# Low weight parts kept in DRAM for the second token half, and weight pieces subtracted in two halves of 256 columns

## The chip, the cores and the metric

The kernel runs on one core of a Trainium2 chip. The metric is the device time of one execution in microseconds (us); three executions of the kernel before took 2840.0, 2847.2 and 2849.79 us, median 2847.2. A core has five engines that run side by side, each through its own instructions in program order: TensorE (PE; its weight loads are shown apart as PEld), VectorE (DVE), ScalarE (ACT), GpSimd (POOL) and SyncE (SP), which here issues every DMA.

## What is computed

One layer of a hybrid encoder trunk over 1024 tokens of width 2048. A combined projection of the normalized input feeds two branches: a recurrent mixer with 16 heads (RWKV-7) and a sparse attention that lets each query see its 256 best-scored keys. Their gated outputs go through an output projection, then a gated update with a side input `p` and a final norm.

```python
def reference(x, p, w_in, norm_g, ...):
    h = x
    xn = rms_norm(h, norm_g[i])
    z = xn @ w_in[i]
    z_rw, g_rw, q_lat, kv_lat, k_idx, w_idx, g_ds = jnp.split(z, splits, axis=-1)
    o_rw = rwkv7_mixer(z_rw, ...)          # state S updated token by token
    o_ds = dsa_mixer(q_lat, kv_lat, k_idx, w_idx, ...)   # top_k(score, 256), softmax over those
    mixed = jnp.concatenate([o_rw * jax.nn.silu(g_rw), o_ds * jax.nn.silu(g_ds)], axis=-1)
    h = h + mixed @ w_out[i]
    h = h + (p[i] @ ple_w[i]) * jax.nn.sigmoid(h @ ple_gate_w[i])
    return rms_norm(h, final_g)
```

## The kernel before

**Split products.** Every large matrix product is taken in three matmuls, so that the fast number format of TensorE (`F32R`) loses nothing: a float32 operand is split into a high part (its rounded copy) and a low part (the difference), and the product is `wh*xh + wh*xl + wl*xh`. `w_piece` (line 507) does this for a weight piece of 128 x 512 values (four blocks of 128 x 128): a DMA loads it into `wr`, ACT makes `wh` by a copy, POOL makes `wl` by a subtraction of 512 columns, and `gemm_part` (line 517) runs twelve matmuls of 128 x 512 on it. `wr` has four buffers and `wh` and `wl` five each (`NWR, NWH`). The weight of the combined projection, `w_z` (46 column tiles of four pieces) with `w_z80` (one narrow tile of four pieces), makes 188 pieces. It goes through `w_piece` twice, once for each half of the tokens (`hf` 0 and 1, 512 tokens each): PE holds the split `x` of one half at a time (`xh`, `xl`).

**Phase 1, to about 1.6 ms.** For each token half, eight units of two heads: `zunit` projects their four tiles (r, k, v, gate), and two steps of 256 tokens each (`sub`, line 960) run the recurrence: `chunk_setup` builds and inverts small triangular matrices on PE, DVE, ACT and POOL, `chunk_serial` walks four chunks of 64 tokens. The steps are a chain, each waiting for the state of the one before. Between them stands work that nobody waits for soon, at the lowest priority (`LF`): in the second half these are `dsa_lat(1)`, the eight gate tiles `gds(j, 1)`, and behind the units the first thirteen tiles of the output projection of the recurrent branch for the first token half, `wout_rw(0)` (`MW`, matmuls on `mh`, `ml`).

**Phase 2, to about 2.27 ms.** It can begin when the last step has left its buffers. `pix` matmuls score all keys for 16 index heads; DVE adds them up in `MK`. Then a search on DVE and ACT halves an interval 31 times for each group of query tiles (`count`, `jk` on DVE and `js` on ACT, line 1146), and `pick_keys` marks the keys. The rest of `wout_rw` (three tiles of the first token half, sixteen of the second) is the work that PE has beside scoring and search. Then come the attention heads in eight pairs `u`, whose logits are the `plg` matmuls; those of query tiles 2 to 7 need the search.

**Phase 3.** The other half of the output projection, the gated update and the norm, again with `w_piece` (`w_o`, `w_pg`, `w_pl`).

**What sets the order.** Nothing is issued as it is written. `Sched` records all operations, and `plan` (line 267) lays them out engine by engine with costs and latencies of its own: the engine that is free first takes the ready operation of the lowest level number (chain of the recurrence 0, weight splits and evacuations 1, scoring 2, projections 3, `LF` 4). A POOL operation with operands in SBUF is planned as one that excludes DVE operations with two such operands, and the other way round (`lock`). Line 382 issues the result, so nearly every instruction of the profile carries that line and is known by its tiles. An engine runs its instructions in that fixed order, whatever the true times are.

Of the kernel before, what the change touches and what calls it, by code (L numbers as in the profile page):

```python
# [10 lines left out]
F32 = mybir.dt.float32  # L11
# [4 lines left out]
OP = mybir.AluOpType  # L16
# [12 lines left out]
LB, LA, LC, LEVAC, LSPLIT, LX, LG, LF, LSQ = 0, 0, 1, 1, 1, 2, 3, 4, 4  # L29
# [356 lines left out]
def hybrid_kernel(ctx, tc, cst, msk, bkt, prm, xt, pt_, w_z, w_z80, w_lora, w_uq, w_iq, w_uk, w_uv, w_o, w_pg,  # L386
                  w_pl, rel_bias, out):
    ctx.enter_context(tc.manual_schedule())
    nc = Sched(tc.nc)
    dram = ctx.enter_context(tc.tile_pool(name="dram", bufs=1, space=DRAM))  # L390
    dt = lambda n, shape: dram.tile(shape, F32, name=n)
# [2 lines left out]
    kid = [dt(f"ki{h}", [64, TH]) for h in range(2)]  # L394
    gdd, h1d = ([[dt(f"{n}{j}_{h}", [128, TH]) for h in range(2)] for j in range(m)] for n, m in (("gd", 8), ("h1", 16)))
    bsk, vbd = dt("bsk", [16, 128, 384]), dt("vb", [16, 384])
    parts = {}

    def pool(stack, keep=None, **kw):
        p_ = Pool(nc, stack.enter_context(tc.tile_pool(**kw)), kw["bufs"])  # L400
# [106 lines left out]
    def w_piece(src, kn, n):  # L507
        wr = wp.tile([128, 4, 128], F32, name="wr", tag="wr", bufs=W_[0])
        nc.sync.dma_start(wr[:, :kn, :n], src.rearrange("p (k n) -> p k n", k=kn))
        with nc.level(LSPLIT):  # L510
            wh = wp.tile([128, 4, 128], F32R, name="wh", tag="wh", bufs=W_[1])
            nc.scalar.activation(wh[:, :kn, :n], wr[:, :kn, :n], AF.Copy)
            wl = wp.tile([128, 4, 128], F32R, name="wl", tag="wl", bufs=W_[1])
            nc.gpsimd.tensor_tensor(wl[:, :kn, :n], wr[:, :kn, :n], wh[:, :kn, :n], op=OP.subtract)
        return wh, wl

    def gemm_part(pz, src, n, k0, kn, nk, xh, xl, w=None):
        wh, wl = w or w_piece(src, kn, n)
        for k in range(kn):
            kk = k0 + k  # L520
            for j, (a, b) in enumerate(((wh, xh), (wh, xl), (wl, xh))):
                nc.tensor.matmul(pz[:n], a[:, k, :n], b(kk), start=(kk == 0 and j == 0),
                                 stop=(kk == nk - 1 and j == 2), skip_group_check=True)
# [16 lines left out]
    def zgroup(tiles, before=lambda g, piece: None):  # L540
        pzs = [pz_tile() for _ in tiles]
        for g in range(4):
            early = []
            before(g, lambda: early.append(w_piece(w_z[tiles[len(early)], g], 4, 128)))
            for j, (pz, i) in enumerate(zip(pzs, tiles)):
                gemm_part(pz, w_z[i, g], 128, g * 4, 4, 16, xh_, xl_, early[j] if early else None)
        return pzs
# [363 lines left out]
    def kept(n, g):  # L911

        if (n, g) in parts:
            pair = []
            for d, nm in zip(parts[n, g], ("wh", "wl")):
                t = wp.tile([128, 4, 128], F32R, name=nm, tag=nm, bufs=W_[1])
                nc.sync.dma_start(t.bitcast(F32), d)
                pair.append(t)
            return pair
        pair = w_piece(w_o[n, g], 4, 128)  # L920
        parts[n, g] = [dt(f"wo{n}_{g}{a}", [128, 4, 128]) for a in "hl"]
        for d, t in zip(parts[n, g], pair):
            nc.sync.dma_start(d, t.bitcast(F32))
        return pair
# [605 lines left out]
```

## Time and profile before

| | us |
|---|---|
| executions timed | 2840.0, 2847.2, 2849.79 |
| median | 2847.2 |
| the profiled execution | 2844.57 |
| its span in the profile | 2842.8 |
| PE busy | 2701.8 (95%) |
| DVE busy | 1644.8 (58%) |
| ACT busy | 1482.0 (52%) |
| POOL busy | 1336.5 (47%) |

The profile is of one execution. Busy time of PE is a union of matmul spans that overlap each other: a stretch that is 100% busy is read for its number of matmuls. The 1.8 us between the profiled execution and its span lie outside the first and last instruction.

### The profile page before, as it was taken

To read this page: it belongs to the slowest core of one execution; us is meant where nothing else is said; L and a number is where in the kernel's file an instruction comes from. 1 tells how busy PE (TensorE), PEld (TensorE's weight loads), DVE (VectorE), ACT (ScalarE), POOL (GpSimd) and SP (SyncE) were. 2 spreads that over 40 slices of the span, in tenths; PEclk is the share of its full clock that TensorE was granted. 3 is DMA by queue.
4 is the path that set the end of the run, shared out by engine and by line. 5 is a ranking of instruction groups with operands and counts; after the bars stand their busy time and mean duration, and the time that the engine had idled before them with its cause. 6 is when DMAs were issued, how large, how long until landed. Compare 5 with 4: busy or idle time off the path is not lost. (4 is left out here: it accounts for less than half of the span.)

```text
span 2842.8 us, 46633 instructions
## 1 busy us (share of the span) xinstructions
PE 2701.8 (95%) x16482; PEld 2157.9 (76%) x16482; DVE 1644.8 (58%) x3709; ACT 1482.0 (52%) x3265; POOL 1336.5 (47%) x1371
## 2 busy tenths in 40 slices
PE   7999999999999999999999999948999999999996
PEld 5777778778778778777877788826776788878885
DVE  6457667546764566667665478987666641135312
ACT  5445555535654355555555466895767533343332
POOL 5545445555455545545555421023334455656654
PEclk9999999999999999999999999968999999999998
DMA  4232222232332222222227844511223343355332
GB/s 159 82 116 70 68 71 75 75 89 71 99 100 84 89 68 68 71 69 70 79 82 240 310 146 137 175 36 39 73 65 90 102 138 97 97 157 174 103 99 92
DMA packets 172586, 293.36 MB, mean 103 GB/s; under 512 B 23440, under 2 KB 44992, under 8 KB 172352
## 3 DMA queue, kind: packets, MB, share of 16 engines
q1 hardware_dynamic: 172352, 290.38, 32.9%
q8 instruction: 130, 2.13, 0.3%
q14 instruction: 104, 0.85, 0.1%
HBM read 232.87 MB, written 52.19 MB: 100 GB/s over the span
## 5 line engine op out<-in xcount | busy, mean ns | idle before, releaser
L382 POOL TENSOR_TENSOR wl<-wr,wh 128x512 fp32r<-128x512 f32 (+1 forms) x624 | 812.8, 1306 | 773.5 <-ACT wh L382 720.4
L382 ACT ACTIVATE wh<-wr 128x512 fp32r<-128x512 f32 (+1 forms) x624 | 384.1, 617 | 731.7 <-PE pz L382 536.1
L382 PE MATMUL pz<-xh,wh 128*128 128x512 f32 (+1 forms) x1504 | 609.5, 407 | 11.5 <-ACT wh L382 7.6
L382 PE MATMUL pz<-xh,wl 128*128 128x512 f32 (+1 forms) x1504 | 610.2, 408 | 2.3 <-POOL wl L382 2.1
L382 PE MATMUL pz<-xl,wh 128*128 128x512 f32 (+1 forms) x1504 | 611.1, 408 | 0.0
L382 PEld LDWEIGHTS pz<-xh,wh 128*128 128x128 f32 (+1 forms) x1504 | 285.6, 190 | 62.5 <-ACT wh L382 9.4
L382 PEld LDWEIGHTS pz<-xh,wl 128*128 128x128 f32 (+1 forms) x1504 | 285.1, 190 | 51.4 <-POOL wl L382 5.5
L382 PEld LDWEIGHTS pz<-xl,wh 128*128 128x128 f32 (+1 forms) x1504 | 285.8, 190 | 45.9 <-DVE xl L382 0.3
L382 DVE SCALAR_TENSOR_TENSOR tg<-tg,pg 128x512 f32<-128x512 f32 x32 | 22.0, 687 | 314.3 <-ACT tg L382 303.1
L382 DVE CAST_PREDICATED QX<-MS,pq 128x512 f16<-128x512 uint8 x160 | 110.3, 689 | 158.7 <-PE pq L382 157.6
L382 PE MATMUL pz<-hh,wh 128*128 128x512 f32 x512 | 199.3, 389 | 0.0
L382 PE MATMUL pz<-hh,wl 128*128 128x512 f32 x512 | 199.3, 389 | 0.0
L382 PE MATMUL pz<-hl,wh 128*128 128x512 f32 x512 | 199.2, 389 | 0.0
L382 POOL TENSOR_TENSOR mb<-mk,bt 128x256 f32<-128x256 f32 (+1 forms) x128 | 89.2, 702 | 153.6 <-DVE mx L382 126.3
L382 ACT ACTIVATE Ztb<-pzt 64x256 f16<-64x256 f32 x320 | 120.6, 377 | 61.3 <-PE pzt L382 55.9
L382 ACT ACTIVATE lgt<-lgt,nm 128x128 f32<-128x128 f32 (+7 forms) x128 | 98.8, 772 | 55.0 <-DVE nm L382 54.2
L382 PE MATMUL ptt<-C,lgt 128*128 128x128 f32 x576 | 99.7, 289 | 23.8 <-ACT lgt L382 22.4
L382 ACT ACTIVATE Sw<-UV,Wx 64x64 f32<-64x64 f32 x240 | 82.2, 342 | 58.9 <-DVE UV L382 55.5
L382 PEld LDWEIGHTS pz<-hh,wh 128*128 128x128 f32 x512 | 96.1, 188 | 20.0
L382 PEld LDWEIGHTS pz<-hl,wh 128*128 128x128 f32 x512 | 96.1, 188 | 20.0
L382 PEld LDWEIGHTS pz<-hh,wl 128*128 128x128 f32 x512 | 96.1, 188 | 19.7
L382 PE MATMUL po<-PT,V 128*64 128x128 f32 x1152 | 87.6, 287 | 18.7 <-ACT PT L382 18.2
(331 smaller groups left out, 6008.3 us busy)
## 6 DMA issues: line engine op xcount, KB each, us to landing
wr<-in_w_z_dram SPq DMA_DIRECT2D x368, 256.0 KB, 2.6
wr<-in_w_pg_dram SPq DMA_DIRECT2D x128, 256.0 KB, 2.6
wr<-in_w_o_dram SPq DMA_DIRECT2D x88, 256.0 KB, 2.9
h<-h SPq DMA_DIRECT2D x60, 256.0 KB, 3.2
h<-in_xt_dram SPq DMA_DIRECT2D x32, 256.0 KB, 3.7
out_dram<-h SPq DMA_DIRECT2D x32, 256.0 KB, 2.3
gd<-gd SPq DMA_DIRECT2D x16, 256.0 KB, 2.3
mix<-m SPq DMA_DIRECT2D x32, 128.0 KB, 1.7
```

Of the source, the lines that this page charges most:

```text
L382: getattr(self.real[o.eng], o.name)(*o.args, **o.kw)
```

## The change

Two edits, both in `w_piece`.

```diff
-    parts = {}
+    parts, lows, KEEP = {}, {}, (w_z.tensor.name, w_z80.tensor.name)
...
             wl = wp.tile([128, 4, 128], F32R, name="wl", tag="wl", bufs=W_[1])
-            nc.gpsimd.tensor_tensor(wl[:, :kn, :n], wr[:, :kn, :n], wh[:, :kn, :n], op=OP.subtract)
+            key = src.tensor.name, src.offset
+            if key in lows:
+                nc.sync.dma_start(wl[:, :kn, :n].bitcast(F32), lows[key])
+                return wh, wl
+            for k in range(0, kn, 2):
+                k_ = slice(k, min(k + 2, kn))
+                nc.gpsimd.tensor_tensor(wl[:, k_, :n], wr[:, k_, :n], wh[:, k_, :n], op=OP.subtract)
+        if src.tensor.name in KEEP:
+            lows[key] = dt(f"low{len(lows)}", [128, kn, n])
+            with nc.level(LF):
+                nc.sync.dma_start(lows[key], wl[:, :kn, :n].bitcast(F32))
         return wh, wl
```

The first time a piece of `w_z` or `w_z80` comes by (first token half), its `wl` is also stored to a DRAM tile of 256 KB, at the lowest level. The second time, `wl` is loaded from there and POOL does nothing for it; `wr` is still loaded and `wh` still made by ACT. All pieces that POOL still subtracts, of every weight with `kn` above 2, are subtracted in two operations of 256 columns each. The matmuls are the same in number and shape.

The planner lays all of this out anew. On POOL, in the second token half, the weight pieces stood between the operations of the recurrence (`IX`, `rsd`, `hr`, `QX`, `BRb`, `rk`, `ALb`, `Wx`). One step before:

```order
L382 TENSOR_TENSOR wl<-wr,wh 128x512 x3
L382 TENSOR_TENSOR IX<-C,QX 128x256
L382 COPY zt<-carry 128x1
L382 TENSOR_TENSOR rsd<-vr,nh 128x4
L382 TENSOR_TENSOR wl<-wr,wh 128x512
L382 TENSOR_TENSOR hr<-hs,nh 128x4
L382 COPY QX<-eye_178 128x512
L382 TENSOR_TENSOR wl<-wr,wh 128x512
L382 TENSOR_TENSOR BRb_218<-r,Wx 64x4x64 x2
L382 TENSOR_TENSOR wl<-wr,wh 128x512 x3
L382 TENSOR_TENSOR rk<-r,kp 128x256
L382 TENSOR_TENSOR wl<-wr,wh 128x512
```

and after:

```order
L382 TENSOR_TENSOR IX<-C,QX 128x256
L382 TENSOR_TENSOR rsd<-vr,nh 128x4
L382 COPY zt<-carry 128x1
L382 TENSOR_TENSOR hr<-hs,nh 128x4
L382 COPY QX<-eye_178 128x512
L382 TENSOR_TENSOR BRb_218<-r,Wx 64x4x64 x2
L382 TENSOR_TENSOR rk<-r,kp 128x256
L382 TENSOR_TENSOR ALb_211<-AB,A16b_217 64x4x64 x2
```

The operations of the recurrence now follow each other with no weight piece between them. On SP, at the same place, each load of a raw piece had no partner before:

```order
L382 DMA wr<-in_w_z_dram 128x512 x7
L382 DMA upr<-in_w_lora_dram 128x256
L382 DMA wr<-in_w_z_dram 128x512 x3
L382 DMA mix_2_69<-m 128x256
L382 DMA wr<-in_w_z_dram 128x512 x15
```

and after:

```order
L382 DMA wl<-low_964 128x512
L382 DMA wr<-in_w_z_dram 128x512
L382 DMA wl<-low_968 128x512
L382 DMA wr<-in_w_z_dram 128x512
L382 DMA upr<-in_w_lora_dram 128x256
L382 DMA wl<-low_1125 128x512
L382 DMA wr<-in_w_z_dram 128x512
```

Loads of `wl` and `wr` alternate; the `wr` behind a `wl` is that of a piece three further on. On PE the change shows at the end of the scoring. Before, the last `pix` matmuls are followed by the output projection of the second token half (`mh_19066`, `mh_19072`), 186 matmuls, up to the first `pg<-CH,hk` of the attention:

```order
L382 MATMUL pz<-mh_19072,wl 128x512
L382 MATMUL pix<-KIH,qs_19036 128x512
L382 MATMUL pix<-KIL,qs_19036 128x512
L382 MATMUL pix<-KIH,qs_19036 128x512
L382 MATMUL pix<-KIL,qs_19036 128x512
L382 MATMUL pz<-mh_19066,wh 128x512
L382 MATMUL pz<-ml_19067,wh 128x512
```

After, the output projection of the first token half (`mh_4064`, `mh_4070`) is not done yet when the scoring ends, and all of the second half's still lies behind it, 538 matmuls up to the same `pg<-CH,hk`:

```order
L382 MATMUL pz<-ml_4071,wh 128x512
L382 MATMUL pix<-KIH,qs_18993 128x512
L382 MATMUL pix<-KIL,qs_18993 128x512
L382 MATMUL pix<-KIH,qs_18993 128x512
L382 MATMUL pix<-KIL,qs_18993 128x512
L382 MATMUL pz<-mh_4070,wl 128x512
L382 MATMUL pz<-mh_4070,wh 128x512
L382 MATMUL pz<-ml_4071,wh 128x512
```

The scoring has moved forward by 352 matmuls in PE's order. In matmuls of the program from its first one, the marks that the next parts use are these:

| mark in PE's order | before | after |
|---|---|---|
| matmuls of one step of the second token half, mean of 13 | 260 | 236 |
| last matmul of the recurrence (`pch`) | 9274 | 8897 |
| first and last `pix` | 9451, 10134 | 9042, 9782 |
| first `pg<-CH,hk` of the attention | 10321 | 10321 |
| first `plg` of head pair 0, of head pair 1, of head pair 2 | 10543, 10727, 10957 | 10543, 10727, 10957 |
| all | 14873 | 14873 |

## Rows read from the trace of the kernel before

**Rows 1.** The page's busy times: us (share of the span) xinstructions.

```profile
PE 2701.8 (95%) x16482; PEld 2157.9 (76%) x16482; DVE 1644.8 (58%) x3709; ACT 1482.0 (52%) x3265; POOL 1336.5 (47%) x1371
```

**Rows 2.** Busy us by stretch (start:end, length; engines; granted TensorE clock, DMA share, GB/s).

```profile
981.00:1519.00 538.00, 535.05 (x3788) 427.83 (x3787) 354.23 (x694) 288.44 (x756) 273.42 (x284) 1.00 0.26 79
1512.00:1628.00 116.00, 109.38 (x622) 87.59 (x621) 61.48 (x109) 49.34 (x117) 58.27 (x52) 0.96 0.84 285
1854.00:1920.00 66.00, 24.75 (x75) 14.56 (x75) 54.82 (x240) 63.93 (x124) 14.83 (x17) 0.58 0.12 31
1959.00:1999.00 40.00, 37.69 (x303) 28.48 (x302) 26.39 (x121) 28.25 (x63) 14.13 (x25) 0.99 0.24 65
2400.00:2500.00 100.00, 100.00 (x442) 82.81 (x442) 11.03 (x16) 34.72 (x60) 59.99 (x49) 1.00 0.32 97
```

**Rows 3.** PE waits, 1854 to 1959 us: who waited for whom, us, times, longest.

```profile
PE plg L382 <- DVE mx L382: 23.7, 11, 5.5
```

**Rows 4.** Timeline of PE: start us, us, operation [idle before <-releaser]; marks.

```profile
981.36 0.20 PE L382 MATMUL pres<-QX,A16b 128*128 128x64 f16 x1
...
1518.92 0.19 PE L382 MATMUL pres<-QX,A16b 128*128 128x64 f16 x1 [0.79 <-DVE QX L382]
...
1776.92 0.40 PE L382 MATMUL pix<-KIL,qs 128*128 128x512 f32 x1
...
1819.33 0.62 PE L382 MATMUL pg<-CH,hk 128*128 128x512 f32 x2
...
1853.87 0.33 PE L382 MATMUL plg<-kh,qs 128*128 128x128 f32 x1 [0.96 <-ACT V L382]
...
1959.13 0.31 PE L382 MATMUL plg<-kh,qs 128*128 128x128 f32 x1
...
1999.24 0.30 PE L382 MATMUL plg<-kh,qs 128*128 128x128 f32 x1 [0.33 <-PE plg L382]
```

**Rows 5.** Timeline of DVE: the first count and the last halving of the search.

```profile
1780.12 0.80 DVE L382 TENSOR_SCALAR_CACHE_REDUCE jk<-mk,th 128x640 f16<-128x640 f32 x1
...
1921.27 0.15 DVE L382 SCALAR_TENSOR_TENSOR th<-xm,th 128x2 uint32<-128x2 uint32 x1
```

**Rows 6.** Groups of DVE, 1780 to 1921 us (xcount | busy us, mean ns | idle before): output projection's evacuations.

```profile
L382 DVE TENSOR_TENSOR h<-pz,h 128x512 f32<-128x512 f32 x8 | 5.5, 688 | 1.0 <-PE pz L382 0.8
```

**Rows 7.** Timelines of POOL, DVE and PE around one step's setup.

```profile
1120.02 0.85 DVE L382 TENSOR_TENSOR KB<-kp,iW 64x256 f32<-64x256 f32 x2
...
1246.47 1.85 DVE L382 TENSOR_TENSOR KB<-kp,iW 64x256 f32<-64x256 f32 x2
...
1246.69 1.34 POOL L382 TENSOR_TENSOR wl<-wr,wh 128x512 fp32r<-128x512 f32 x1 [1.07 <-ACT wh L382]
1247.98 0.93 POOL L382 TENSOR_TENSOR rk<-r,kp 128x256 f32<-128x256 f32 x1
...
1252.08 1.05 PE L382 MATMUL pA<-ARb,KB 128*128 128x128 f32 x8
```

**Rows 8.** Groups of DVE and POOL, 981 to 1519 us: busy us, mean ns | idle before.

```profile
L382 DVE TENSOR_TENSOR ARb<-kkn,Wx 64x256 f32<-64x256 f32 x26 | 22.7, 872 | 1.5 <-ACT Wx L382 1.1
L382 DVE SCALAR_TENSOR_TENSOR KB<-q,iW 64x256 f32<-64x256 f32 x26 | 20.7, 795 | 0.3
L382 DVE TENSOR_TENSOR KB<-kp,iW 64x256 f32<-64x256 f32 x26 | 18.1, 697 | 0.2
...
L382 POOL TENSOR_TENSOR wl<-wr,wh 128x512 fp32r<-128x512 f32 x130 | 170.9, 1315 | 187.3 <-ACT wh L382 174.4 <-PE pv L382 4.1 <-PE pch L382 2.6
```

**Rows 9.** Groups of POOL, 2300 to 2800 us: weight pieces of both widths.

```profile
L382 POOL TENSOR_TENSOR wl<-wr,wh 128x512 fp32r<-128x512 f32 x165 | 223.6, 1356 | 168.4 <-ACT wh L382 168.0
...
L382 POOL TENSOR_TENSOR wl<-wr,wh 128x256 fp32r<-128x256 f32 x32 | 25.2, 786 | 36.4 <-ACT wh L382 36.4
```

**Rows 10.** DMA issues: transfer, count, KB each, median us from issue to landing.

```profile
wr<-in_w_z_dram SPq DMA_DIRECT2D x368, 256.0 KB, 2.6
...
lraw<-qn SPq DMA_DIRECT2D x6, 256.0 KB, 5.3
```

## Prediction

> **What bounds the kernel now.** I read the busy times first: PE is busy for 95% of the span and no other engine for more than 58% [rows 1]. That is a mean, so I went on to the table by stretch. In phase 3, PE runs 442 matmuls in 100 us, none idle [rows 2]: a 128 x 512 matmul costs 100/442 = 0.226 us where nothing holds it. In the thirteen steps of the second token half, PE is idle for 3 us of 538 [rows 2]. Time is lost elsewhere: from 1854 to 1920 us PE is busy for 24.75 us of 66, at a granted clock of 0.58, between its two levels of 1.2 and 2.4 GHz, while ACT is busy for 63.9 and DVE for 54.8 [rows 2]. What PE waits for there is the logits' evacuation on DVE, among others 23.7 us before `plg` [rows 3]; DVE is at the search.
>
> The marks in PE's timeline put times to this [rows 4]. The last scoring matmul starts at 1776.92, the attention's first projection at 1819.33, the first `plg` of head pair 0 at 1853.87, of pair 1 at 1959.13, of pair 2 at 1999.24. Pair 0 has 184 matmuls in the order of the program and takes 105.3 us; pair 1 has 230 and takes 40.1. The search begins at 1780.12 and its last halving is done at 1921.27, 141 us later [rows 5]. So the kernel is bound by PE nearly everywhere, and by the search from about 1854 to 1959. PE's work in that hole cannot be had earlier: pair 0 needs the keys, and the output projection that filled PE beside the scoring and the search has run out by 1819. **A gain can come from here alone**: the search must start earlier against PE's work.
>
> **What the change does there.** PE's order says where the search stands. Up to the mark `pg<-CH,hk` both programs have the same 10321 matmuls, but the last scoring matmul is followed by 538 of them instead of 186. If PE is held up no more than before, that mark stays at 1819.33. The 186 took 1819.33 - 1776.92 = 42.4 us, 0.228 each [rows 4]; 538 take 122.7, so the scoring ends at about 1697 and the search starts at 1700, 80 us earlier.
>
> The search gets a little longer, because more of the output projection now runs beside it: 352 more matmuls are 14.7 tiles of 24, each with an addition of 0.69 us on DVE [rows 6], 10 us; and ACT has to split some 17 weight pieces that it had done before, at about that price again, 12 us. If the two overlap, the search takes 153 us and ends at 1853; one after the other, 163 us and 1863. PE reaches pair 0's first `plg` at 1853.87 as before, and now finds the thresholds made.
>
> Pair 0 then costs what it needs itself. At pair 1's pace its 184 matmuls take 184 x 40.1/230 = 32.1 us, and pair 1 starts at 1886: the good end. From the end of the search to the start of pair 1 the kernel before took 1959.13 - 1921.27 = 37.9 us, in which DVE picked the keys of query tiles 5 to 7; but the tiles ahead had been done while it searched. If nothing of the 32.1 and the 37.9 overlaps, pair 1 starts at 1854 + 32 + 38 = 1924: the bad end. I take 1899, the end of the search at 1853 plus 37.9 and a quarter of the 32.1, since steady pairs leave DVE a third of the time free [rows 2]. So pair 1 starts 1959 - 1899 = **60 us earlier**, between 35 and 73. From there on PE's order is the same.
>
> **Can the steps keep that pace?** This is the condition. The scoring moves forward because the thirteen steps that took (1518.92 - 981.36)/13 = 41.35 us [rows 4] now have 236 matmuls instead of 260: 24 x 0.226 = 5.4 us less, 35.9 us per step, with nothing of the lowest level left between them. A chain that needs longer makes PE wait. What the change takes out of the chain are eight pieces of POOL per step. A pair of `KB` operations on DVE takes 0.85 us alone, and 1.85 where it met a `wl` of 1.34 us [rows 7]; POOL's own `rk` began when that `wl` ended. In the groups over 13 steps, `ARb` and both `KB` take 872, 795 and 697 ns instead of 425 [rows 8]: two of each per step, 2 x (447 + 370 + 272) = 2.2 us. `wl` is 170.9 us of POOL's 273.4 busy in this stretch [rows 2, 8], so 63% of that, 1.4 us, should go. POOL's operations behind a `wl` gain up to 1.3 us each; at one or two places of the chain that is 1.3 to 2.6. Together 2.7 to 4.0 us of the 5.4. The rest must be slack, and there is some: the last `KB` above ended at 1246.47 + 1.85 = 1248.32 and its reader `pA` started at 1252.08, 3.8 us later [rows 7], held by PE's order alone. I take 5 us of new waits over the fifteen steps; the ends are none and 2 us per step, 30 us.
>
> **The rest of the change.** Two halves in place of 512 columns: a subtraction of 256 columns takes 786 ns, one of 512 takes 1356 [rows 9], so a piece costs up to 2 x 786 - 1356 = 0.22 us more. It stays hidden, since a piece feeds PE for 12 x 0.226 = 2.7 us and POOL needs 1.6; were POOL the bound, 400 pieces would cost 88 us. For the start the first half comes sooner, worth under 1 us. The stores, 188 of 256 KB in some 870 us, are 55 GB/s beside 79 at a DMA share of 0.26 [rows 2]; the loads, eight in 36 us, 57 GB/s. Either brings the share to about 0.45: hidden. On SP a store waits for POOL's `wl` and the next `wr` stands behind it, but that `wr` waits for the same `wl` now, to get its buffer. A `wl` load waits for PE to leave the fifth piece back, so it has four pieces, 4 x 2.7 = 10.8 us, to land; transfers of this size land in 2.6 us in the median and the slowest kind in 5.3 [rows 10].
>
> The sum: 2844.6 - 60 + 5 = 2789.6 for the profiled execution; the median of the three runs lies 2.6 above that execution, so **2792**. Ends of this case: 2844.6 - 73 + 2.6 = 2774, and with the smaller gain and half of the 30 us, 2844.6 - 35 + 15 + 2.6 = 2827.
>
> **The rivals.**
>
> *PE outruns the chain* (slower). If the steps still need 41.35 us, PE waits 5.4 us in each of fifteen, 81 us, in the middle of work that nothing else can fill, and gets 60 back later: 2847 + 21 = 2868. It decides from 60/15 = 4.0 us per step, which means that the chain would have lost only 1.4 us. For it: the part that I can count, 2.7 to 4.0, is less than 5.4. Against it: the slack in rows 7. Half of it, 2 to 3 us per step, gives 2817 to 2832.
>
> *The search stays late.* ACT is busy 63.9 of 66 us in the search's second half [rows 2], and the splits of moved pieces come on top. If it ends at 1885, pair 1 starts at 1885 + 38 = 1923, and 2844.6 - 36 + 5 + 2.6 = 2816.
>
> *`wl` comes late from DRAM.* The widest stretch of DMA work, 1512 to 1628, has a share of 0.84 at 285 GB/s, and PE idles 6.6 us of 116 in it [rows 2]. The same kind of stretch with twice the loads for the gate tiles could double that: 2799. It needs landings over 10.8 us to grow further, twice the slowest seen. The Trainium skill (DMA: Bandwidth & Descriptors, "Latency and other measured facts") gives HBM's access latency as 0.2 us on average and 2 us at high load; an estimate from that page would be a landing of 2.6 + 1.8 = 4.4 us, the row of 5.3 is already slower than this, and neither reaches 10.8. By that rule too this rival moves the time by little.
>
> *Nothing changes.* PE is the bound and keeps its matmuls; if the search did not end earlier, or pair 0 were held by something that I don't see, the time stays at 2847.
>
> **How the numbers follow.** My case, 2774 to 2827 around 2792: 0.72. The late search, around 2816: 0.07, and a partly outrun chain, 2817 to 2832: 0.06; both are faster than before. Late `wl`: 0.03, still faster. Nothing: 0.05. An outrun chain beyond 4 us per step: 0.07. A measurement here tells 0.3%, 8.5 us, from no change. Faster by more than that: 0.72 + 0.07 + 0.06 + 0.03, less 0.02 of my case and its neighbours that end between 2838 and 2856, 0.86; within: 0.07; slower: 0.07. The range from 2775 to 2828 leaves out the two cases of no gain, 0.12, and the outer parts of the others, some 0.08.
>
> **What would show it.** Right: scoring over near 1700, the search done near 1853, pair 0 in 40 to 50 us instead of 105 with a granted clock near 1, the steps at 36 us with PE hardly idle, `KB` and `ARb` near 425 to 600 ns in the second token half. Wrong: steps over 38 us with PE waiting for `KB`, `QX` or `UV` from DVE or ACT, or for `wl` from a DMA; a search that ends after 1870; or pair 0 still over 80 us long.

## The result and the profile after

The changed kernel takes 2779.8 us in the median of four executions (2777.72 to 2781.48), the kernel before, run beside it, 2847.36 (2840.0 to 2849.79): a ratio of 0.9767, 95% interval 0.9747 to 0.9786. That is 67.6 us less, 12.6 more than the 55 that were forecast. The profiled execution took 2779.27 us, its span is 2777.5.

The page's busy times of the changed kernel, to be read against [rows 1]:

```profile
PE 2681.9 (97%) x16482; PEld 2147.7 (77%) x16482; DVE 1557.8 (56%) x3709; ACT 1488.0 (54%) x3265; POOL 1191.9 (43%) x1587
```

POOL has lost 145 us of work and PE none of its matmuls, yet it is PE that finishes sooner: the span is 65.3 us shorter, of which 45.4 us are PE's idle time and 19.9 us its busy time. The stretches of [rows 2] in the changed kernel, with the same columns (the third one is now the stretch of the search):

```profile
981.00:1519.00 538.00, 534.02 (x3891) 426.64 (x3891) 331.61 (x748) 304.18 (x801) 110.90 (x162) 1.00 0.42 132
1512.00:1628.00 116.00, 109.17 (x485) 88.42 (x484) 81.45 (x85) 76.58 (x121) 61.61 (x53) 0.97 0.66 217
1692.00:1828.00 136.00, 131.99 (x588) 107.31 (x587) 125.65 (x485) 118.50 (x210) 23.76 (x23) 1.00 0.79 265
1854.00:1920.00 66.00, 57.01 (x407) 42.66 (x407) 54.48 (x195) 43.04 (x93) 32.63 (x39) 0.95 0.21 59
```

The same columns for the search of the kernel before, then for head pair 0 before and after:

```profile
1780.00:1921.00 141.00, 95.48 (x474) 76.33 (x473) 127.39 (x520) 128.86 (x242) 20.83 (x23) 0.80 0.32 101
1854.00:1959.00 105.00, 52.20 (x226) 34.28 (x227) 88.75 (x348) 81.27 (x158) 31.40 (x33) 0.63 0.09 23
1848.00:1893.00 45.00, 37.09 (x227) 26.82 (x228) 39.35 (x126) 26.61 (x57) 27.59 (x29) 0.93 0.19 54
```

Three things stand there. PE is busy for 132.0 of the 136 us of the search, where it was for 95.5 of 141 before. From 1854 to 1920 it runs 407 matmuls at a granted clock of 0.95 where it ran 75 at 0.58 [rows 2]: the hole is gone. And of the 60 us by which pair 0 is shorter, 45 are idle time of PE; the other 15 are busy time of the same matmuls, at a granted clock of 0.93 instead of 0.63. The marks of [rows 4 and 5] in PE's and DVE's timeline (start us, us, operation):

```profile
1688.50 0.39 PE L382 MATMUL pix<-KIL,qs 128*128 128x512 f32 x1
...
1813.66 0.62 PE L382 MATMUL pg<-CH,hk 128*128 128x512 f32 x2
...
1847.94 0.33 PE L382 MATMUL plg<-kh,qs 128*128 128x128 f32 x1 [0.69 <-ACT V L382]
...
1892.90 0.31 PE L382 MATMUL plg<-kh,qs 128*128 128x128 f32 x1
```

```profile
1692.33 0.80 DVE L382 TENSOR_SCALAR_CACHE_REDUCE jk<-mk,th 128x640 f16<-128x640 f32 x1
...
1827.79 0.15 DVE L382 SCALAR_TENSOR_TENSOR th<-xm,th 128x2 uint32<-128x2 uint32 x1
```

Head pair 0 takes 1892.9 - 1847.9 = 45.0 us instead of 105.3. Pair 1 starts 66.2 us earlier than before; 60.3 of that is pair 0, 5.9 was there already at 1847.9. From pair 1 to the end it takes 884.6 us, before 883.6.

The table gives the same marks for all kernels below. The experiments ran in three later rounds, in which the kernel before took 2848.89 us (`e1` to `e4`), 2850.87 (`e5` to `e8`) and 2848.51 (`e9` to `e12`); the ratios of the experiments are to these. "Step" is the mean of the same thirteen steps of the second token half as in the prediction, from the first `pres` of each; "PE idle" is PE's idle time in them.

| kernel | median us | step | PE idle | search | pair 0 | pair 1 starts |
|---|---|---|---|---|---|---|
| before | 2847.4 | 41.35 | 2.9 | 1780.1 to 1921.3 | 105.3 | 1959.1 |
| after | 2779.8 | 35.81 | 2.1 | 1692.3 to 1827.9 | 45.0 | 1892.9 |
| `e1_kept_whole` | 2802.6 | 35.79 | 2.1 | 1711.8 to 1845.9 | 45.0 | 1918.0 |
| `e2_halves_only` | 2839.0 | 40.69 | 2.7 | 1770.3 to 1912.0 | 95.2 | 1950.8 |
| `e3_half_kept` | 2792.4 | 37.51 | 1.2 | 1712.3 to 1852.6 | 47.2 | 1905.5 |
| `e4_told_quick` | 2842.4 | 38.62 | 30.0 | 1742.0 to 1881.5 | 45.1 | 1954.2 |
| `e5_before_16` | 2795.4 | 41.35 | 3.0 | 1779.5 to 1863.7 | 54.2 | 1907.2 |
| `e6_after_16` | 2778.6 | 35.92 | 3.2 | 1696.1 to 1772.0 | 43.8 | 1892.7 |
| `e7_pool_sub` | 2829.1 | 38.44 | 24.0 | 1752.4 to 1885.9 | 47.0 | 1938.7 |
| `e8_pool_set` | 2801.2 | 36.86 | 8.8 | 1725.0 to 1862.1 | 46.9 | 1914.7 |
| `e9_store_whole` | 2859.8 | 41.34 | 2.9 | 1795.9 to 1937.5 | 105.4 | 1975.3 |
| `e10_late_store` | 2799.8 | 35.79 | 2.1 | 1701.3 to 1834.9 | 46.6 | 1908.6 |
| `e11_halves_stored` | 2786.7 | 35.80 | 2.1 | 1693.8 to 1831.3 | 45.0 | 1903.4 |
| `e12_quarters` | 2777.5 | 35.79 | 2.1 | 1688.5 to 1823.6 | 45.1 | 1887.7 |

### The profile page after: what moved, and what is told of

It is laid out like the page before. It is cut to its first block, busy times and chain, and to the rows that moved or that the text cites. A ratio compares the mean times of both kernels' runs of the same rounds, so it can differ in the third digit from the quotient of the medians.

```text
span 2777.5 us, 47623 instructions
## 1 busy us (share of the span) xinstructions
PE 2681.9 (97%) x16482; PEld 2147.7 (77%) x16482; DVE 1557.8 (56%) x3709; ACT 1488.0 (54%) x3265; POOL 1191.9 (43%) x1587
## 5 line engine op out<-in xcount | busy, mean ns | idle before, releaser
L382 POOL TENSOR_TENSOR wl<-wr,wh 128x256 fp32r<-128x256 f32 (+1 forms) x840 | 663.5, 811 | 471.6 <-ACT wh L382 437.3
L382 DVE SCALAR_TENSOR_TENSOR mk<-rl,WI,mk 128x384 f32<-128x384 f32 (+2 forms) x90 | 95.8, 1105 | 16.5 <-ACT rl L382 16.2
L382 ACT ACTIVATE PT<-ptt 128x512 f32<-128x512 f32 (+1 forms) x160 | 81.7, 549 | 40.4 <-PE ptt L382 39.4
```

The costliest lines, as they stand in the source:

```text
L382: getattr(self.real[o.eng], o.name)(*o.args, **o.kw)
```

## Experiments: the two parts of the change apart

**`e1_kept_whole`: keep the low parts, subtract whole.**

```diff
-            for k in range(0, kn, 2):
-                k_ = slice(k, min(k + 2, kn))
-                nc.gpsimd.tensor_tensor(wl[:, k_, :n], wr[:, k_, :n], wh[:, k_, :n], op=OP.subtract)
+            nc.gpsimd.tensor_tensor(wl[:, :kn, :n], wr[:, :kn, :n], wh[:, :kn, :n], op=OP.subtract)
```

> The low parts are kept in DRAM as in the changed kernel, but POOL subtracts each piece whole, in one operation of 512 columns. PE's order has a step of 236 matmuls in the second token half, as with both edits, and the last scoring matmul at 9765 instead of 9782. Theory (the kept low parts alone take the recurrence's steps from 41 to 36 us, the search then starts early enough): the time is that of both edits, 2772 to 2788 us. Rival (shorter holds of POOL in the first token half and in the last phase matter too): 2790 us or more.

Measured: 2802.63 us, 0.9835 of before (0.982 to 0.985): the rival came true. That is 22.8 us behind the changed kernel by the medians, 19 by the two ratios. **`e2_halves_only`** is the other part alone:

```diff
-    parts, lows, KEEP = {}, {}, (w_z.tensor.name, w_z80.tensor.name)
+    parts, lows, KEEP = {}, {}, ()
```

> The two halves alone: nothing is kept in DRAM, POOL subtracts all 624 pieces, in halves. PE's order has a step of 258 matmuls instead of 260, and the last scoring matmul at 10082 instead of 10134. Theory: the search starts 52 x 0.228 = 12 us earlier and gives back about that, 2833 to 2840 us. Rival (the halves do nothing): 2845 to 2850. Rival (the halves carry a good part of the gain, because DVE gets in between them): below 2820.

Measured: 2838.99 us, 0.9968 (0.9955 to 0.9981): about 9 us better than before, as its theory had it. So the halves are worth 9 us where nothing is stored and some 20 (19 to 23) where low parts are stored, and the two parts don't add up: by the ratios -47 and -9, together -66, each uncertain by some 5 us; the traces, further below, say the same. In the prediction the halves were worth nothing. Beside the kept parts they do not work in the second token half: step and pair 0 of `e1_kept_whole` are those of the changed kernel. They work in the first one, which the runs further below take up.

**`e3_half_kept`: keep every second weight block only.**

```diff
-        if src.tensor.name in KEEP:
+        if src.tensor.name in KEEP and key[1] // 65536 % 2 == 0:
```

> Both edits, but only every second piece of each weight tile is kept; POOL subtracts the others in the second token half as well. PE's order has a step of 245 matmuls, and the last scoring matmul at 9859, 275 matmuls earlier than in the kernel before. Theory (the gain is the earlier search, and saturates when PE's work fills it): the search starts 275 x 0.228 = 63 us earlier; the hole in head pair 0 closes nearly as far as with all pieces kept, 2785 to 2798 us. Rival (every piece taken off POOL is worth the same, some 0.36 us): half of the gain, 2810 to 2817.

Measured: 2792.39 us, 0.9798 (0.9783 to 0.9812). Half of the pieces brings 2.0 of the 2.3% that all of them bring. The step falls by 3.8 of the 5.5 us, and pair 0 is down to 47.2 already: once the search ends before PE reaches pair 0, an earlier search makes pair 0 hardly shorter. Of the 12.6 us by which its pair 1 starts later than in the changed kernel, 10.4 are there when pair 0 starts; they arise beside the search (set side by side by the number of PE's record, the trace is 2 us ahead of the changed kernel's at record 10000 and 10 us behind at 11500).

## Experiments: is it the search?

**`e5_before_16` and `e6_after_16`: 16 halvings instead of 31**, in the kernel before and in the changed one.

```diff
-        for bit in range(30, -1, -1):
+        for bit in range(30, 14, -1):
```

> The kernel before with 16 halvings of the search instead of 31: the last 15 are left out, so the keys are only roughly the best 256. The search is shorter by 15/31 of its 141 us, some 66 us. Theory (the hole in head pair 0 is the search): pair 0 gets shorter by nearly that, down to some 40 to 45 us from 105, and the time falls to 2783 to 2795 us. Rival (the hole is something else, such as the picking of keys or the restart of the attention): over 2820.

> The changed kernel with the same 15 halvings left out. Theory (in the changed kernel the search ends before PE needs it, so its length costs next to nothing): 2768 to 2778 us, at most 12 us less than with all 31. Rival (the search still bounds): about 2720 to 2750.

Measured: 2795.43 us, 0.9804 (0.9775 to 0.9832), and 2778.56 us, 0.9745 (0.9716 to 0.9773). Both leave out the last 15 halvings and mark other keys, so they are no versions to use. In the kernel before, with its step of 41.35 us and its search from 1779.5 untouched but for its length, the shorter search (to 1863.7) takes pair 0 from 105.3 to 54.2 us, where 40 to 45 had been expected; the time is 0.4 us above the expected range. The stretch 1854 to 1920 of `e5_before_16`, columns as in [rows 2]:

```profile
1854.00:1920.00 66.00, 50.65 (x312) 36.37 (x311) 54.58 (x199) 40.83 (x85) 31.50 (x34) 0.87 0.22 53
```

312 matmuls stand where [rows 2] had 75. In the changed kernel the same edit ends the search 56 us earlier, at 1772.0, and gains 1.2 us by the medians; the intervals of the two ratios overlap, so it is not told from nothing. So the late search was the price of the kernel before, and the changed kernel doesn't pay it any more.

## Experiments: why do the steps keep the pace?

PE has 24 matmuls fewer per step, and the chain of the recurrence must need 5.4 us less or have slack. **`e4_told_quick`** gives the kernel before nearly the changed order and no relief: its planner is told that the subtractions of the second token half cost 0.05 us and exclude nothing on DVE.

```diff
+            key = src.tensor.name, src.offset
+            if key in seen:
+                nc.ops[-1].cost, nc.ops[-1].lock = 0.05, False
+            seen.add(key)
```

> The kernel before, with nothing kept and no halves, but the planner is told that the 188 subtractions of the second token half take 0.05 us and hold nobody. PE's order is then that of the changed kernel: a step of 236 matmuls, the last scoring matmul at 9756. On the chip POOL still needs 1.3 us for each. Theory (the chain itself has to get shorter): PE outruns it, the steps stay over 38 us with PE waiting, 2810 to 2865 us. Rival (the order alone makes the gain, the chip's chain had the slack all along): 2775 to 2792 us.

Measured: 2842.42 us, 0.9972 (0.996 to 0.9985). The order alone closes the hole (pair 0 takes 45.1 us) and gives nearly all of it back ahead of it, as the first rival said: the step takes 38.62 us, and PE idles for 30 us in thirteen of them. What PE waits for there (who waited for whom, us, times, longest; 970 to 1480 us):

```profile
PE pch L382 <- DVE UV L382: 14.0, 10, 2.6
PE pch L382 <- DVE rh L382: 5.7, 6, 1.4
PE pA L382 <- DVE KB L382: 2.7, 5, 0.7
```

Of the 5.5 us by which the step of the changed kernel is shorter, this one has 41.35 - 38.62 = 2.7 without any relief: that much was slack. The other 2.8 come from POOL's relief. Two kernels split those. Both are the changed kernel with work put back on POOL which the planner doesn't reckon with, into a raw piece whose content is dead. Only the next use of its buffers has to wait for it: SP's loads into `wr`, about equally in both (182 and 185 us from 981 to 1480), and in the first kernel, whose operation reads `wh` too, ACT for 5.6 us, 0.4 per step. **`e7_pool_sub`** reads two operands, as the removed subtraction did:

```diff
+                nc.gpsimd.tensor_tensor(wr[:, :kn, :n], wr[:, :kn, :n], wh[:, :kn, :n], op=OP.subtract)
+                nc.ops[-1].cost, nc.ops[-1].lock = 0.05, False
                 return wh, wl
```

> The changed kernel, in which POOL does the subtraction of 512 columns in the second token half all the same, into the raw piece that nobody reads any more; PE gets its low part from DRAM. The planner is told that this costs 0.05 us and holds nobody, so PE's order has steps of 237 matmuls. Nobody waits for the result. If POOL's operation itself slows the chain (by holding DVE up and by standing ahead of POOL's own steps), the steps go to 38 to 42 us and the time to 2810 to 2865 us. If it was PE's or the buffers' wait for the low part that mattered, the steps stay at 36 us and the time at 2780 to 2800.

**`e8_pool_set`** keeps POOL about as long with three fills (`MEMSET`), which read nothing:

```diff
+                for a in (slice(0, 4), slice(0, 4), slice(0, 2)):
+                    nc.gpsimd.memset(wr[:, a, :], 0.0)
+                    nc.ops[-1].cost = 0.02
                 return wh, wl
```

> As the run with the subtraction that nobody reads, with the same order on PE, but POOL writes zeros into the dead raw piece instead, in three memsets of together 1.3 us that read nothing. If the price lies in holding DVE out while POOL reads two operands, the steps stay near 36 us and the time at 2780 to 2805 us. If it lies in POOL's queue, its own steps of the chain standing behind the piece, the time is about that of the run with the subtraction.

Measured: 2829.11 us, 0.9922 (0.9893 to 0.9951), with the subtraction; 2801.24 us, 0.9824 (0.9796 to 0.9853), with the fills. Groups of DVE and POOL from 981 to 1480 us (busy us, mean ns | idle before), first of `e7_pool_sub`, then of `e8_pool_set`, then DVE of the changed kernel:

```profile
L382 POOL TENSOR_TENSOR wr<-wr,wh 128x512 f32<-128x512 f32 x105 | 137.5, 1310 | 147.0 <-ACT wh L382 118.9 <-issue 23.2 <-POOL BRb L382 3.0
L382 DVE TENSOR_TENSOR ARb<-kkn,Wx 64x256 f32<-64x256 f32 x26 | 22.0, 845 | 0.3
L382 DVE SCALAR_TENSOR_TENSOR KB<-q,iW 64x256 f32<-64x256 f32 x26 | 18.2, 698 | 0.3
L382 DVE TENSOR_TENSOR KB<-kp,iW 64x256 f32<-64x256 f32 x26 | 16.8, 645 | 0.3
```

```profile
L382 POOL MEMSET wr<- 128x512 f32 x218 | 115.7, 531 | 148.6 <-ACT wh L382 119.9 <-issue 14.2 <-POOL BRb L382 6.7
L382 POOL MEMSET wr<- 128x256 f32 x109 | 34.5, 317 | 6.3
L382 DVE TENSOR_TENSOR ARb<-kkn,Wx 64x256 f32<-64x256 f32 x28 | 18.2, 650 | 0.6 <-ACT wh L382 0.3
L382 DVE TENSOR_TENSOR KB<-kp,iW 64x256 f32<-64x256 f32 x28 | 14.7, 523 | 0.4
L382 DVE SCALAR_TENSOR_TENSOR KB<-q,iW 64x256 f32<-64x256 f32 x28 | 13.3, 474 | 0.3
```

```profile
L382 DVE TENSOR_TENSOR KB<-kp,iW 64x256 f32<-64x256 f32 x26 | 16.8, 646 | 0.4
L382 DVE TENSOR_TENSOR ARb<-kkn,Wx 64x256 f32<-64x256 f32 x26 | 15.4, 591 | 0.6
L382 DVE SCALAR_TENSOR_TENSOR KB<-q,iW 64x256 f32<-64x256 f32 x26 | 11.3, 434 | 0.3
```

The fills keep POOL busy for 150 us, the subtraction for 138. Yet the step takes 36.86 us with the fills and 38.44 with the subtraction, and 35.81 with neither. So of 2.6 us per step 1.05 are POOL's being occupied, which delays its own operations (PE waits 4.4 us for `rk`), and 1.6 come on top where POOL's operation reads two operands from SBUF (at most 0.4 of them ACT's wait for `wh`): beside it DVE's three groups are 122 to 224 ns longer than beside the fills. (`KB<-kp` is as long in the changed kernel, with no weight piece about: 24 of its 26 overlap POOL's `rk`, which reads two operands too, and take 665 ns in the mean; the other two take 422.) The fills are three short operations where the subtraction is one long one, but that is not what makes the difference, as one `KB` beside each shows, first of `e7_pool_sub`, then of `e8_pool_set` (start us, us):

```profile
1300.09 1.32 POOL L382 TENSOR_TENSOR wr<-wr,wh 128x512 f32<-128x512 f32 x1 [1.00 <-POOL BRb L382]
1300.17 1.51 DVE L382 SCALAR_TENSOR_TENSOR KB<-q,iW 64x256 f32<-64x256 f32 x1
...
1315.77 0.53 POOL L382 MEMSET wr<- 128x512 f32 x1 [0.20 <-POOL BRb L382]
1315.86 0.42 DVE L382 SCALAR_TENSOR_TENSOR KB<-q,iW 64x256 f32<-64x256 f32 x1
```

Of the operations of the three groups, 40 overlap fills and nothing else of POOL: they take 418 ns in the mean and 425 at most, and 417 with POOL idle. The 18 that overlap the subtraction alone take 1111 ns in the mean, up to 1552. The Trainium skill (SBUF — State Buffer, "SBUF: two separate sides") says that a DVE operation with two SBUF inputs and a GpSimd operation that reads SBUF lock each other out for a whole instruction. These two runs agree: what costs DVE the time is that POOL's operation reads, not that POOL is busy.

## Experiments: why are whole subtractions slow beside stores?

PE's order in `e1_kept_whole` and in the changed kernel has nearly the same counts, though not the same sequence, so that a difference at one record can be off by some us. Setting the two traces side by side by the number of PE's record shows where the 23 us between the medians arise: `e1_kept_whole` is behind by 3.8 us at record 400, 6.1 at 1600, 15.9 at 2800, 21.7 at 4800, and then stays between 20 and 28 to the end, where it is 22. Record 4800 is reached at 751 us in the changed kernel: nearly all of the loss lies in the first token half, where the stores are. Three kernels ask what the stores do there.

**`e9_store_whole`: the stores alone,** with whole subtractions and no loads of kept parts.

```diff
             key = src.tensor.name, src.offset
-            if key in lows:
-                nc.sync.dma_start(wl[:, :kn, :n].bitcast(F32), lows[key])
-                return wh, wl
...
-        if src.tensor.name in KEEP:
+        if src.tensor.name in KEEP and key not in lows:
```

> The stores alone: every weight piece subtracted whole, stored in the first token half, and never loaded again (POOL subtracts it a second time in the second half). Theory A, a store costs time only where the subtraction ahead of it is long: the first token half takes some 14 us longer than in the kernel before, as with everything kept and whole subtractions, and nothing is gained later: 2860 to 2866. Rival B, the loss of that run came from something in the changed order of the second half: the time stays at that of before, 2845 to 2852.

Measured: 2859.81 us, 1.0041 of before (1.0025 to 1.0056). The stores cost 11 us, just under what theory A gave, and all of it in the first half: the trace is 15 us behind that of before at record 4800 and 16 to 17 at the end. Ten of the 15 are idle time of PE (34.0 us in its first 4800 records, before 23.7), in few places. At one of the largest a raw piece lands 6.3 us after its issue at 366.99, ACT stands for it, and the recurrence stands for ACT:

```profile
373.30 0.63 ACT L382 ACTIVATE wh<-wr 128x512 fp32r<-128x512 f32 x1 [3.00 <-DMA wr<-in_w_z_dram]
373.95 0.22 ACT L382 ACTIVATE UV<-pch 64x64 f32<-64x64 f32 x1
...
374.23 0.49 PE L382 MATMUL pch<-UV,KBT 128*128 128x128 f32 x2 [2.66 <-ACT UV L382]
```

**`e10_late_store`: whole subtractions, and a planner that counts a store as ready 3 us later,** so that SP issues other loads ahead of it.

```diff
-        return LAT.get((d.eng, self.eng), 0.0) if d.eng != self.eng or self.deps[j] else 0.0
+        return self.late + LAT.get((d.eng, self.eng), 0.0) if d.eng != self.eng or self.deps[j] else 0.0
...
                 nc.sync.dma_start(lows[key], wl[:, :kn, :n].bitcast(F32))
+                nc.ops[-1].late = 3.0
```

> Whole subtractions, stored and loaded, but the planner counts a store as ready 3 us later, so that SP issues other loads ahead of it. Theory A1, the loss of the whole subtractions is loads of raw pieces that stand on SP behind a store that waits for POOL: the first half comes back to the pace of before, and the time falls from 2803 to 2785 to 2791; ACT's waits for raw pieces fall from 41 us towards 22 in 100 to 900 us. Rival A2, what costs is the whole subtraction itself (DVE and ACT held up by it, buffers held longer by the store): 2800 to 2806.

Measured: 2799.83 us, 0.9829 (0.9815 to 0.9844). As a time that is at the edge of A2's range, 2.8 us below `e1_kept_whole` and not told apart from it; A1's range is missed by 9 us. The trace of the first token half shows what A1 expected there. Two lines each of `e1_kept_whole`, `e10_late_store` and the changed kernel, 100 to 760 us: the stretch with its columns, then ACT's splits (busy us, mean ns | idle before, and what ended it):

```profile
100.00:760.00 660.00, 647.34 (x4368) 512.65 (x4367) 395.31 (x767) 330.85 (x842) 329.35 (x353) 0.99 0.47 142
...
L382 ACT ACTIVATE wh<-wr 128x512 fp32r<-128x512 f32 x156 | 97.6, 629 | 154.1 <-PE pz L382 82.5 <-DMA wr<-in_w_z_dram 35.0 <-issue 11.3
```

```profile
100.00:760.00 660.00, 650.26 (x4454) 515.77 (x4453) 404.40 (x785) 338.76 (x867) 331.62 (x356) 1.00 0.47 144
...
L382 ACT ACTIVATE wh<-wr 128x512 fp32r<-128x512 f32 x156 | 97.5, 629 | 145.2 <-PE pz L382 87.3 <-DMA wr<-in_w_z_dram 18.7 <-issue 10.5
```

```profile
100.00:760.00 660.00, 653.90 (x4516) 519.41 (x4515) 396.28 (x800) 344.38 (x881) 365.37 (x519) 1.00 0.47 144
...
L382 ACT ACTIVATE wh<-wr 128x512 fp32r<-128x512 f32 x157 | 98.7, 630 | 151.8 <-PE pz L382 96.9 <-DMA wr<-in_w_z_dram 19.9 <-POOL wl L382 14.1
```

Read the counts of PE and the wait for `wr`, with the other kernels:

| 100 to 760 us | matmuls | ACT's idle before `wh`, for `wr` |
|---|---|---|
| before | 4475 | 20.5 |
| `e2_halves_only` | 4512 | 19.1 |
| `e9_store_whole` | 4363 | 39.6 |
| `e1_kept_whole` | 4368 | 35.0 |
| `e10_late_store` | 4454 | 18.7 |
| after | 4516 | 19.9 |

A matmul of this stretch is worth 660/4516 = 0.146 us. Halves without stores bring 37 matmuls, 5 us. Stores behind whole subtractions cost 107, 16 us, and raw pieces come late to ACT; in the order with later stores the pieces are in time again, and 86 of the 107 are back. Stores behind halves cost nothing that this stretch shows (4512, 4516).

That the loads are held up on SP behind a store, as A1 has it, the traces do not show. A raw piece needs one of four buffers, so it can't be issued before the subtraction four pieces back has ended. It is issued 0.04 us after this end in the mean in the kernel before, 0.14 in `e1_kept_whole`, 0.05 in `e10_late_store`, and 0.22 in the changed kernel, which loses nothing (100 to 760 us). SP stands before stores for 130 us in `e1_kept_whole` and for 127 in the changed kernel, and the order is the same in both: a piece's store goes out when the loads of three or four further raw pieces have been issued, in `e10_late_store` four or five. What does become worse beside stores is how long a raw piece takes to land: more than 4 us for 3 of 158 before, 18 of 157 in `e9_store_whole`, 14 in `e1_kept_whole`, 8 of 158 in `e10_late_store`, but 15 of 159 in the changed kernel too. So it stays open by what way the stores cost 16 us, and why halves protect from it. Nor does `e10_late_store` change the order on SP alone: the planner lays out all engines anew, and of PE's first 4800 records only 2401 stand at the same place as in `e1_kept_whole`.

Open too is where the median of `e10_late_store` leaves the 11 us that its trace has regained at record 4800. In that trace 9.5 are still there when pair 1 starts; the rest of the program then takes 885.6 us beside 881.8 in the trace of `e1_kept_whole`, the shortest of all of them, and the profiled execution is the fastest of its four (2796.18 to 2801.48). One execution's parts scatter by some us, and a difference of this size between medians is no more than that.

**`e11_halves_stored`: halves for the stored pieces of the first token half only,** whole subtractions for all other weights.

```diff
-            for k in range(0, kn, 2):
-                k_ = slice(k, min(k + 2, kn))
+            cut = 2 if src.tensor.name in KEEP else 4
+            for k in range(0, kn, cut):
+                k_ = slice(k, min(k + cut, kn))
```

> As the changed kernel, but halves only for the stored pieces of the combined projection in the first token half; all other weights are subtracted whole. Theory A, the gain of the halves lies in the first token half alone: 2777 to 2783, as the changed kernel. Rival, a part of the 23 us lies behind it, in phases 2 and 3 where 212 pieces and more are subtracted: 2785 to 2800.

Measured: 2786.72 us, 0.9782 (0.9765 to 0.9798), 6.9 above the changed kernel; the intervals of the two ratios overlap. By its time it is in the rival's range, but not told from the changed kernel. In the traces 4 us of the distance arise in the first 110 us, where both kernels have the same order on PE, so that is scatter; some 6 arise about the search, where the orders differ. By the medians some 16 of the 23 us therefore belong to the stored pieces; whether the rest belongs to the other weights isn't settled.

**`e12_quarters`: four subtractions of 128 columns,** as a version that might be better.

```diff
-            for k in range(0, kn, 2):
-                k_ = slice(k, min(k + 2, kn))
+            for k in range(0, kn):
+                k_ = slice(k, k + 1)
```

> As the changed kernel, with four subtractions of 128 columns a piece. If the gain of the halves is the time for which one POOL operation keeps others waiting, quarters give some more in the first token half, up to half of what the halves alone gave there (9 us): 2773 to 2778. If a fixed price per operation eats it (786 ns for 256 columns against 1356 for 512 leaves some 0.2 us per operation), POOL needs about 2.0 us a piece beside 2.7 of PE: the same or slower, 2780 to 2800.

Measured: 2777.48 us, 0.9758 (0.9739 to 0.9776): in the range of the first theory, but not to be told from the changed kernel. Its subtractions from 100 to 760 us, and those of the changed kernel:

```profile
L382 POOL TENSOR_TENSOR wl<-wr,wh 128x128 fp32r<-128x128 f32 x615 | 288.2, 498 | 113.4 <-ACT wh L382 95.5 <-DMA bsk<-vb 6.9 <-DMA wr<-in_w_z_dram 3.0
```

```profile
L382 POOL TENSOR_TENSOR wl<-wr,wh 128x256 fp32r<-128x256 f32 x311 | 238.2, 785 | 184.8 <-ACT wh L382 164.6 <-DMA bsk<-vb 5.3 <-PE pz L382 5.3
```

A piece costs POOL 4 x 498 = 1.99 us instead of 1.57. Its trace is 10 us ahead of the changed kernel's at record 4800, and 5.2 when pair 1 starts. But 7.5 of the 10 are there at record 400 already, where `e11_halves_stored` differed by 4.3 with the same order, so it isn't shown that shorter subtractions still pay in the first half.

## Why the prediction was right, and where not

**Right in its main line.** The gain comes from the hole in pair 0, because the search starts earlier against PE's work. The step was put at 35.9 us, and took 35.81 with PE idle for 2.1 us in thirteen. `e5_before_16` shows most of the gain, 55 us, without the change, and `e6_after_16` that nothing measurable of it is left.

**Pair 0 was put at 45 us (1854 to 1899), and took 45.0, by luck.** The 1899 were counted from the end of the search: 37.9 us, and a quarter of the 32.1 that pair 0 would need at pair 1's pace. Measured, the search ends 20 us before PE reaches pair 0, and pair 1 starts 65 us after it, not 46. What takes 45 us is pair 0 itself: 37.1 us of busy PE, and waits of which 6.0 are for DVE (1847 to 1893 us; us, times, longest):

```profile
PE plg L382 <- DVE mx L382: 3.2, 5, 1.8
PE pg L382 <- DVE qs L382: 2.8, 2, 2.0
```

In `e6_after_16`, with the search over 77 us before pair 0, it still takes 43.8. So the term for pair 0's own work was too small, and the wait behind the search, which made up for it, was not paid.

**The scoring ended at 1688.9, not at 1697, and the first `pg<-CH,hk` came 5.7 us earlier, not 5 later.** The term that failed is "hidden", said of the two halves and of the stores: both put the first token half at what it took. It became 8.0 us shorter (record 4800). Without these 8, the mark would have come 2.3 us later than before, so the new waits are some 2 us where 5 were taken. In the first-half runs the two terms fail in opposite ways: the halves gain 9 us, and the stores cost 15 where subtractions are whole. That the next `wr` waits for the same `wl` in any case holds in the traces (0.14 us behind it in `e1_kept_whole`); it did not follow that the stores are free. Two errors of opposite sign, of which the change happens to pay only the good one: that is luck as well.

**The search took 135.5 us, not 153.** Both of its additions went wrong. The 12 us for some 17 splits of weight pieces were wrong: from 1692 to 1828 us ACT makes 7 of them, since most pieces of the output projection have been stored split by this time, as the kernel before does too (`wl<-wo_0l` and `wo_1h<-wh`, 16 of each in its DMAs). The 10 us for DVE were there, but not in the way:

```profile
L382 DVE TENSOR_TENSOR h<-pz,h 128x512 f32<-128x512 f32 x23 | 15.7, 688 | 5.1 <-PE pz L382 4.1 <-issue 0.8
```

23 additions instead of 8 [rows 6], and DVE is still idle for 10 of the 136 us. And the search of before held a wait that I had not looked for, ACT standing for DVE at its start; in the changed kernel this wait is 0.3 us. That it makes up the difference no run shows. From the waits of the kernel before, 1779 to 1922 us:

```profile
ACT js L382 <- DVE js L382: 8.0, 1, 8.0
```

**The sum.** Pair 1 was put at 1959.1 - 60 + 5 = 1904.1 and starts at 1892.9, 11.2 earlier; the rest took 1.0 us more than before. That is 2844.57 - 66.2 + 1.0 = 2779.4 for the profiled execution, measured 2779.27, where 2789.6 was forecast; the median lies 0.5 above it, not 2.6.

**The steps' account.** The relief on DVE was put at 1.4 us per step. (The eight pieces per step are those of the new order; [rows 8] has 130 in thirteen steps, ten each. The sum goes by the busy time and isn't touched.) The three groups of [rows 8] went from 872, 795 and 697 ns to 591, 434 and 646: 2 x 0.693 = 1.39 us. `e7_pool_sub` beside `e8_pool_set` puts a price of 1.6 us on it in the step. The rest of the 5.4 us "must be slack"; `e4_told_quick` shows 2.7 us of it, and that without relief PE idles for 30 us in thirteen steps, as the first rival had it; the time would then be that of before, not above it.

**The loads of kept parts** stay hidden as argued. From the list of DMA issues (count, KB each, median us to landing), and the stretch 1512 to 1628 above, in which PE idles 6.8 us, before 6.6:

```profile
wr<-in_w_z_dram SPq DMA_DIRECT2D x368, 256.0 KB, 2.9
low<-wl SPq DMA_DIRECT2D x184, 256.0 KB, 3.2
wl<-low SPq DMA_DIRECT2D x184, 256.0 KB, 2.6
```

A kept `wl` lands as quickly as a raw piece did [rows 10], against 10.8 us that it has, and in the second token half the DMA share is 0.42 where 0.45 was estimated.

## What to carry to other kernels

Follow a serial block's start through the order of the bound engine: here POOL lost 145 us of work and PE no matmul, and the gain was that a search began while PE still had something else to do. A store that looks hidden by its bandwidth can still cost time, here 11 us at a DMA share of 0.47, so run it alone before calling it free. Ask of two edits that come together what each is worth alone; here -47 and -9 made -66. And compare a forecast term by term: a length that comes out exactly can be two errors.

## What was not expected of the hardware

- A subtraction on POOL of 512 columns takes 1.31 us and three fills together 1.38; the first costs the chain 1.6 us per step more than the second, since it reads two operands from SBUF while DVE does: a DVE operation of 417 ns takes 418 beside a fill and 1111 in the mean beside a subtraction.
- Cutting a POOL operation in two costs it 19% (2 x 785 ns for the 1315 of [rows 8]), in four 51% (4 x 498). The cut in two still made the kernel faster, by 9 us with no other edit; that the shorter hold of POOL is the reason is not shown by a run of its own.
- 256 KB stores of 3.2 us each, at a DMA share of 0.47, cost nothing that the first token half shows behind halves; behind whole subtractions they cost 16 us, four fifths of which (86 of 107 matmuls) one trace regains in the order with later stores. Holding up the raw loads behind them on SP is not how: these are issued 0.14 us after their buffer can be free.
